# Gate/up of a decoder trunk in float32 halves: one product for both parts of h, sums on ACT and DVE; first scores on 64 rows; mask on the diagonal

## The chip, the cores and the metric

One core of a Trainium2 chip runs the kernel. The metric is device microseconds of one execution, the median of several runs. Engines are written as in the profile: PE (TensorE, matmul), PEld (its weight load), DVE (VectorE), ACT (ScalarE), POOL (GpSimd), SP (SyncE, which issues most DMAs).

## What is computed

A trunk of two layers on 256 tokens of width 1024. Each layer is half-step SwiGLU FFN, token mixer, half-step SwiGLU FFN; the mixer of the first layer is MoBA attention with a relative bias, that of the second is MLA attention. Every sub-layer has an RMS norm and a shift, a scale and a gate that come from `c`.

```python
def swiglu(h, w_gate, w_up, w_down):
    return (jax.nn.silu(h @ w_gate) * (h @ w_up)) @ w_down

for layer in range(DEPTH):                       # DEPTH = 2
    mods = c_act @ ada_w[layer] + ada_b[layer]   # 9 vectors of D_MODEL = 1024
    sh1, sc1, g1, sh2, sc2, g2, sh3, sc3, g3 = jnp.split(mods, 9, axis=-1)
    h = modulate(rms_norm(x, norm_g[layer, 0]), sh1, sc1)
    x = x + 0.5 * g1[:, None, :] * swiglu(h, ...)        # D_FF = 2816
    h = modulate(rms_norm(x, norm_g[layer, 1]), sh2, sc2)
    mix = moba_attention(h, ...) if layer < N_A_LAYERS else mla_attention(h, ...)
    x = x + g2[:, None, :] * mix
    h = modulate(rms_norm(x, norm_g[layer, 2]), sh3, sc3)
    x = x + 0.5 * g3[:, None, :] * swiglu(h, ...)
```

With 256 keys MoBA has one block, so each query sees all keys up to its own. Its heads are 64 wide, those of MLA 96 (query and key).

## The kernel before

**Numbers in two parts.** Weights arrive as float32 (`raw`), and `split` makes a high part `hi` (ACT, L628) and the rest `lo` (DVE, L629), both of type float32r, 128x1024 at a time. `h` is kept likewise as `hh` and `hl`. A product is three matmuls, high by high, high by low, low by high (`mm3`, L758 to L760), summed in PSUM. Weights stream from memory once, through three `raw` buffers and eight `hi` and `lo` each.

**An FFN** (`ffn`). The first 512 of the 2816 hidden columns are done with tokens as output rows and 512 moving weight columns (L905; in the first FFN of all, a routine `first` does 768 columns in its own way). The others go in blocks of 128 hidden columns ("blocks" from here on): the weights are the stationary operand, `h` of all 256 tokens moves, and gate and up of one block fill the two halves of one PSUM buffer `mm` (L934 to L940, with `mm3` once for each of 8 slices `k` of the width). There are 16 such blocks in the first FFN and 18 in each of the other three. `units` then takes SiLU of gate (ACT, L887), multiplies by up (DVE, L888) and splits the result into `gh` and `gl` (L773, L774). Down follows, in two halves of 512 output columns, with `gh`, `gl` stationary.

**Adaptation** (`ada_cols`, `ada_gate`). The shift, scale and gate vectors need 160 tiles of 128x1024 (`adaw`, three buffers), each loaded by SP and taken by one DVE operation: L639 for shift and scale, L677 for gates. They run beside everything else.

**Attention** (`attention`). Four heads at a time. MoBA: q and k are transposed; `qz` holds q for even and odd heads apart, with zeros on the other head's 64 rows, so that a score product runs over 128 rows (L989). Scores of 128 queries by 128 or 256 keys are written side by side into PSUM, bias is added and the row maximum found (L1003), then exponentials, transposition, and the product with v (L1045). MLA: the mask is put into PSUM first by a product of `ident_b` and `masks[t]` (L987), 512 columns, and the scores add to it.

**PSUM.** Eight buffers of 128x512: four `mm`, three `tr` (transpositions and attention, name `at`), one `ada`.

**What sets the order.** The program is written in one order, with attention steps and adaptation interleaved by a clock that `pe` advances. Then `Order` re-arranges each engine's queue: it plays the program through with a duration for each instruction (`duration`) and takes on each engine the ready one that is needed first; on PE it takes program order, except for what has been ready long. The queues on the chip run in the order so found, each engine strictly in its own.

The profiled line numbers are those of the functions below.

Of the kernel before, what the change touches and what calls it, by code (L numbers as in the profile page):

```python
# [197 lines left out]
def duration(i, aps):  # L198
# [5 lines left out]
    if e == "PE":  # L204
# [3 lines left out]
        if i.is_transpose:  # L208
            c = 109.0
        elif dt == F32R:  # L210
            c = max(256, cols) / 2.4 + 13.3
        elif dt == F32:
            c = 114.0 if aps[-1].ap[0][1] == DH else 2 * max(112.0, cols / 1.2 + 2.5)
        else:
            c = max(29.0, cols / 2.4 + 7.0)
# [307 lines left out]
def trunk(ctx: ExitStack, tc: tile.TileContext, a: dict, out: bass.AP):  # L523
# [305 lines left out]
    def split_h(h, c0, n, z):  # L829
        cs = slice(c0, c0 + n)  # L830
        h[2].update(range(c0 // P, (c0 + n) // P))
        return split_evac(h[0][:, cs], h[1][:, cs], z)
# [9 lines left out]

    def new_h(t):
        if t == 0:
            pair[:] = [hp.tile([P, NT, D], F32R, tag=g, name=nm(g)) for g in ("hh", "hl")]
        return pair[0][:, t, :], pair[1][:, t, :], set(), list(pair)

    def hk(h, k):
        until(lambda: k in h[2])
        return kslice(h[0], k), kslice(h[1], k)  # L850

    def hk_both(h, k):
        for t in range(NT):
            until(lambda: k in h[t][2])
        return [x[:, :, k * P:(k + 1) * P] for x in h[0][3]]
# [20 lines left out]
    def ffn(layer, idx, h, after, ada_to, start=None):  # L876

        last = (layer, idx) == (1, 1)
        with ExitStack() as st:
# [4 lines left out]
            def units(f, ps):  # L884

                g = gp.tile([P, NT, P], F32, tag="gT", name=nm("g"), bufs=2)
                nc.scalar.activation(g, ps[:, 0], AF.Silu)  # L887
                nc.vector.tensor_tensor(g, ps[:, 1], g, op=ALU.mult)  # L888
                gh, gl = [gq.tile([P, NT, P], F32R, tag=f"{nme}{f}", name=nm(nme)) for nme in ("gh", "gl")]
                split_evac(gh, gl, g)  # L890
                for t in range(NT):
                    gT[f, t] = gh[:, t, :], gl[:, t, :]

            if start:
                start(units)
# [3 lines left out]
            for t in range(0 if start else NT):  # L899
# [10 lines left out]
                g = gp.tile([P, FB], F32, tag="g", name=nm("g"), bufs=2)  # L910
# [13 lines left out]
            for f0 in range(B1 * P if start else FB, F, S):  # L924
# [45 lines left out]
    UNITS = [(0, [0, 1, 2, 3]), (1, [0, 1]), (1, [2, 3])]  # L970

    def attention(ap, g, qTs, kTs, vs, bias, oT, state, after_s=None):
# [4 lines left out]
        pT, ss, sms = {}, [], []  # L977

        def scores():
            until(lambda: state.get("av", 0) >= g)  # L980
            banks = []
            for t, es in UNITS:
                nk = P * (t + 1)
                ps = at_tile()
                ps3 = ps.rearrange("p (e k) -> p e k", k=nk)
                if bias is None:
                    nc.tensor.matmul(ps, ident_b, masks[t], start=True, stop=False)  # L987
                for i, e in enumerate(es):
                    nc.tensor.matmul(ps3[:, i, :], qTs(e, t), kTs(e, nk), start=bias is not None,  # L989
                                     stop=bias is not None or i == len(es) - 1)  # L990
                banks.append(ps3)
            pe(3.0)
            mxs = []
            for (t, es), ps3 in zip(UNITS, banks):
# [3 lines left out]
                if bias is None:  # L998
                    nc.vector.tensor_reduce(mx[:, :len(es)], ps3, axis=AX.X, op=ALU.max, negate=True)
                else:  # L1000
                    for i, e in enumerate(es):
                        s2, ps2 = [x[:, i, :].rearrange("p (b c k) -> p b c k", c=P // NB, k=NB) for x in (s3, ps3)]
# [4 lines left out]
            for u, (t, es) in enumerate(UNITS):  # L1007
                sm = small([P, 4], "sm")
                for i in range(len(es)):
                    nc.scalar.activation(ss[u][:, i, :], (banks if bias is None else ss)[u][:, i, :], AF.Exp,  # L1010
# [614 lines left out]
```

## Time and profile before

| | |
|---|---|
| runs | 1011.45, 1012.14, 1011.46 us; median 1011.46 |
| the profiled execution: span from first to last instruction | 1009.8 us |
| PE / DVE / ACT / POOL busy | 997.3 / 805.0 / 586.9 / 83.7 us |
| DMA | 260.65 MB, 258 GB/s on average |
| first FFN / MoBA / second FFN | about 0 to 225 / 225 to 335 / 335 to 530 us |
| third FFN / MLA / last FFN | about 530 to 714 / 714 to 820 / 820 to 1009 us |

The profile's only clock is that span; the time of a run also holds what lies around it, here 1.7 us against the median. "Busy" counts an instruction from start to end; matmuls overlap each other, so their cost is read from the distance of their starts.

### The profile page before, as it was taken

What the parts mean: (1) busy time and instruction counts of PE and PEld (TensorE: products, weight loads), DVE (VectorE), ACT (ScalarE), POOL (GpSimd) and SP (SyncE); (2) the same over time, 40 slices, a digit from 0 to 9 for tenths busy, and PEclk for the clock granted to TensorE, in tenths of its full rate; (3) what the DMA queues carried; (4) which work ended last, traced back from release to release, by engine and by line L of the source; (5) the groups of instructions that cost most, each with busy time, mean ns of one, the idle gap of its engine ahead of it and who ended that gap; (6) DMA issues with size and microseconds to landing.
All of it is one profiled execution on the core that took longest, in us unless ns stands there. A gap on an engine that the chain in (4) does not pass through costs nothing.

```text
span 1009.8 us, 17261 instructions
## 1 busy us (share of the span) xinstructions
PE 997.3 (99%) x6678; PEld 899.6 (89%) x6678; DVE 805.0 (80%) x1303; ACT 586.9 (58%) x1029; POOL 83.7 (8%) x124
## 2 busy tenths in 40 slices
PE   8999999999999999999999999999999999999998
PEld 6999998888888799998888999988888889999986
DVE  8999988799888999888799886544998788555542
ACT  5688454378765855455367555543879695555421
POOL 3011000022230000000000000000143010000000
PEclk9999999999999999999999999999999999999999
DMA  9989999899787599998988985562343467544630
GB/s 353 403 294 319 384 336 344 284 338 336 268 287 249 217 330 367 324 315 314 340 321 323 339 298 180 176 210 104 105 151 126 167 247 283 180 167 168 221 133 21
DMA packets 54243, 260.65 MB, mean 258 GB/s; under 512 B 6289, under 2 KB 6801, under 8 KB 35986
## 3 DMA queue, kind: packets, MB, share of 16 engines
q1 hardware_dynamic: 52850, 256.06, 69.6%
q0 software_dynamic: 1024, 3.17, 1.1%
q8 instruction: 52, 0.85, 0.3%
q10 hardware_dynamic: 288, 0.33, 0.1%
q14 instruction: 29, 0.24, 0.1%
HBM read 255.34 MB, written 4.19 MB: 257 GB/s over the span
## 4 chain that ended last, share of the span: by engine, by line
PE 91%; DVE 5%; DMA 2%; ACT 0%; issue 0%; SPq 0%; POOL 0%; DVEq 0%; ACTq 0%
PE mm L758 28%; PE mm L759 27%; PE mm L760 27%; PE at L989 2%; DMA raw<-in_first_dram 1%; PE at L1045 1%; PE at L1025 1%; DVE lo L629 1%; PE tr L1146 1%; PE tr L808 1%; DMA adaw<-in_ada_dram 1%; DVE adaw L639 0%; DVE z L824 0%; DVE wlo L1564 0%; DVE hv L1080 0%
## 5 line engine op out<-in xcount | busy, mean ns | idle before, releaser
L629 DVE TENSOR_TENSOR lo<-raw,hi 128x1024 fp32r<-128x1024 f32 (+3 forms) x312 | 370.8, 1202 | 120.2 <-ACT hi L628 119.6
L628 ACT ACTIVATE hi<-raw 128x1024 fp32r<-128x1024 f32 (+3 forms) x312 | 321.2, 1040 | 178.2 <-PE mm L760 126.0
L759 PE MATMUL mm<-hl,hi 128*128 128x256 f32 x1120 | 314.4, 283 | 0.0
L760 PE MATMUL mm<-hh,lo 128*128 128x256 f32 x1120 | 314.0, 283 | 0.0
L758 PE MATMUL mm<-hh,hi 128*128 128x256 f32 x1120 | 313.3, 284 | 0.0
L759 PEld LDWEIGHTS mm<-hl,hi 128*128 128x128 f32 x1120 | 214.2, 192 | 0.5
L760 PEld LDWEIGHTS mm<-hh,lo 128*128 128x128 f32 x1120 | 213.8, 192 | 0.8 <-DVE lo L629 0.2
L758 PEld LDWEIGHTS mm<-hh,hi 128*128 128x128 f32 x1120 | 213.0, 192 | 1.0 <-ACT hi L628 0.2
L639 DVE CUSTOM_DVE_ANT_0 adaw<-adaw,c_b,cols 128x1024 f32<-128x1024 f32 x112 | 140.5, 1281 | 0.7 <-DMA adaw<-in_ada_dram 0.7
L758 PE MATMUL mm<-hi,gh 128*128 128x512 f32 x352 | 137.4, 390 | 0.0
L760 PE MATMUL mm<-hi,gl 128*128 128x512 f32 x352 | 137.1, 390 | 0.0
L759 PE MATMUL mm<-lo,gh 128*128 128x512 f32 x352 | 137.1, 389 | 0.0
L758 PE MATMUL mm<-hi,hh 128*128 128x512 f32 (+1 forms) x240 | 94.7, 400 | 0.6 <-ACT hh L773 0.6
L760 PE MATMUL mm<-hi,hl 128*128 128x512 f32 (+1 forms) x240 | 92.4, 392 | 1.6 <-DVE hl L774 1.6
L887 ACT ACTIVATE g<-mm 128x256 f32<-128x256 f32 x74 | 28.1, 382 | 112.8 <-PE mm L760 112.8
L759 PE MATMUL mm<-lo,hh 128*128 128x512 f32 (+1 forms) x240 | 92.8, 392 | 0.0
L760 PEld LDWEIGHTS mm<-hi,gl 128*128 128x128 f32 x352 | 66.1, 188 | 13.7
L758 PEld LDWEIGHTS mm<-hi,gh 128*128 128x128 f32 x352 | 66.1, 188 | 13.2
L759 PEld LDWEIGHTS mm<-lo,gh 128*128 128x128 f32 x352 | 66.1, 188 | 13.2
L677 DVE SCALAR_TENSOR_TENSOR acc<-adaw,cols,acc 128x1024 f32<-128x1024 f32 x48 | 61.8, 1288 | 0.1
L888 DVE TENSOR_TENSOR g<-mm,g 128x256 f32<-128x256 f32 x74 | 31.2, 421 | 29.6 <-ACT g L887 29.5
L760 PEld LDWEIGHTS mm<-hi,hl 128*128 128x128 f32 x240 | 45.1, 188 | 10.5 <-DVE hl L774 2.1
(226 smaller groups left out, 1216.7 us busy)
## 6 DMA issues: line engine op xcount, KB each, us to landing
raw<-in_w_dram SPq DMA_DIRECT2D x142, 1024.0 KB, 6.0
adaw<-in_ada_dram SPq DMA_DIRECT2D x160, 512.0 KB, 6.0
raw<-in_first_dram SPq DMA_DIRECT2D x24, 256.0 KB, 7.7
raw<-in_w_dram SPq DMA_DIRECT2D x12, 512.0 KB, 3.5
raw<-in_w_dram SPq DMA_DIRECT2D x6, 576.0 KB, 3.7
bias_d<-bt SPq DMA_DIRECT2D x12, 256.0 KB, 5.0
bg<-bias_d POOLq DMA_DIRECT2D x4, 768.0 KB, 6.5
raw<-in_w_dram SPq DMA_DIRECT2D x2, 768.0 KB, 4.4
```

Of the source, the lines that this page charges most:

```text
L628: nc.scalar.activation(hi, src, AF.Copy)
L629: nc.vector.tensor_tensor(lo, src, hi.bitcast(F32), op=ALU.subtract)
L639: nc.vector.tensor_tensor_reduce(wt, wt, c_b, 1.0, cols[:, i, c:c + 1], op0=ALU.mult, op1=ALU.add, accum_out=m_cols[:, i, c:c + 1])
L677: nc.vector.scalar_tensor_tensor(acc, ada_tile(j, k), cact[:, k:k + 1], acc, op0=ALU.mult, op1=ALU.add)
L758: nc.tensor.matmul(ps, lh, rh, start=start, stop=False)
L759: nc.tensor.matmul(ps, lh, rl, start=False, stop=False)
L760: nc.tensor.matmul(ps, ll, rh, start=False, stop=stop)
L808: nc.tensor.transpose(kslice(pt, j), kslice(y, j), ident)
L887: nc.scalar.activation(g, ps[:, 0], AF.Silu)
L888: nc.vector.tensor_tensor(g, ps[:, 1], g, op=ALU.mult)
L989: nc.tensor.matmul(ps3[:, i, :], qTs(e, t), kTs(e, nk), start=bias is not None, stop=bias is not None or i == len(es) - 1)
L1025: nc.tensor.transpose(kslice(pt, i * (t + 1) + kb), ss[u][:, i, kb * P:(kb + 1) * P], ident)
```

## The change

Five things are done together.

1. `h` becomes one tile `[P, KD, 2, NT, P]`: for each slice `k` the high part of all 256 tokens and then the low part, 512 columns in a row. In a block the high weights meet all 512 at once (L955), so that the left half of a PSUM buffer gets high by high and the right half high by low; then the low weights meet the high part of `h` and add to the right half (L962). Gate and up now have a PSUM buffer each. ACT copies the right half out (L966), DVE adds the left half (L967).
2. In all FFNs but the first, two blocks share a tile `both`: SiLU (L969), product (L970) and split are done once for the pair, on 512 columns. In the first FFN blocks stay single, and their tile is `ry`, of which there is one.
3. The first scores (MoBA): `qz` and its zeros are gone; q and k of a head are read from their own 64 partitions, so a product runs over 64 rows. Scores of even and odd heads go to different PSUM buffers (`sides`), four in all; the fourth is the `ada` buffer. Softmax groups are (0, 2) and (1, 3) instead of (0, 1) and (2, 3).
4. MLA: the mask is one tile of four 128x128 diagonals, added behind the scores and only on the diagonal block.
5. `duration` counts an fp32 product as single when its rows or its output partitions are at most 64, as double otherwise, and `Order` plans with that and with the new program.

```diff
+    def views(x, t):
+        return x[:, :, 0, t, :], x[:, :, 1, t, :], set(), x
+
     def new_h(t):
         if t == 0:
-            pair[:] = [hp.tile([P, NT, D], F32R, tag=g, name=nm(g)) for g in ("hh", "hl")]
-        return pair[0][:, t, :], pair[1][:, t, :], set(), list(pair)
+            pair[:] = [hp.tile([P, KD, 2, NT, P], F32R, tag="h", name=nm("h"))]
+        return views(pair[0], t)
...
+            def unit(f, ps):
+                g = tp.tile([P, S], F32, tag="y", name=nm("g"), bufs=4).rearrange("p (n t q) -> p n t q", n=1, t=NT)
+                nc.scalar.activation(g[:, 0], ps[:, 0], AF.Silu)
+                nc.vector.tensor_tensor(g[:, 0], ps[:, 1], g[:, 0], op=ALU.mult)
+                units(f, g)
...
+                n = 1 if start else 2
                 for f in range(f0 // P, (f0 + S) // P):
-                    ps = mm_tile().rearrange("p (i t q) -> p i t q", i=2, q=P)
+                    j = (f - f0 // P) % n
+                    if not j:
+                        both = (tp.tile([P, 512], F32, tag="ry", name=nm("ry"), bufs=1) if start else
+                                sumsp.tile([P, 1024], F32, tag="both", name=nm("both")))
+                        both = both.rearrange("p (i n t q) -> p i n t q", i=2, t=NT, q=P)
                     for i, pl in enumerate(parts):
+                        ps = mm_tile()
                         for k in range(KD):
                             if len(pl) <= k:
                                 pl += nextw()
-                            mm3(ps[:, i], *[w[:, f * P - f0:(f + 1) * P - f0] for w in pl[k]],
-                                *hk_both(h, k), start=k == 0, stop=k == KD - 1)
+                            wh = pl[k][0][:, f * P - f0:(f + 1) * P - f0]
+                            nc.tensor.matmul(ps, wh, hk_both(h, k).rearrange("p i t q -> p (i t q)"),
+                                             start=k == 0, stop=False)
+                            pe(0.227)
...
-                    units(f, ps)
+                        for k in range(KD):
+                            wl = pl[k][1][:, f * P - f0:(f + 1) * P - f0]
+                            nc.tensor.matmul(ps[:, S:], wl, hk_both(h, k)[:, 0].rearrange("p t q -> p (t q)"),
+                                             start=False, stop=k == KD - 1)
+                            pe(0.12)
+                        sums = both[:, i, j].rearrange("p t q -> p (t q)")
+                        nc.scalar.activation(sums, ps[:, S:], AF.Copy)
+                        nc.vector.tensor_tensor(sums, sums, ps[:, :S], op=ALU.add)
+                    if j == n - 1:
+                        nc.scalar.activation(both[:, 0], both[:, 0], AF.Silu)
+                        nc.vector.tensor_tensor(both[:, 0], both[:, 0], both[:, 1], op=ALU.mult)
+                        units(f - j, both[:, 0], n)
...
+                sides = [at_tile() for _ in range(3)] + [ps_ada.tile([P, 512], F32, tag="ada", name=nm("at"))]
+                sides = [x.rearrange("p (e k) -> p e k", k=P * (i // 2 + 1)) for i, x in enumerate(sides)]
+                for t in range(NT):
+                    for e in range(GH):
+                        nc.tensor.matmul(sides[2 * t + e % 2][:, e // 2, :], qTs(e, t), kTs(e, P * (t + 1)),
+                                         start=True, stop=True)
...
+                    for i, e in enumerate(es):
+                        nc.tensor.matmul(ps3[:, i, :], qTs(e, t), kTs(e, P * (t + 1)), start=i == 0, stop=False)
+                    nc.tensor.matmul(ps3[:, :, t * P:], ident_b, mask[:, :len(es)], start=False, stop=True)
...
+                def half(x, e, n0, n1):
+                    return x[e % 2 * DH:(e % 2 + 1) * DH, e // 2, n0:n1]
```

**PE, gate/up in the first FFN.** One block's gate, as PE's queue holds it before: three matmuls of 256 columns for each `k` (out, then moving operand and weights).

```order
L758 MATMUL mm_1566<-hh_109,hi_1112 128x256
L759 MATMUL mm_1566<-hl_110,hi_1112 128x256
L760 MATMUL mm_1566<-hh_109,lo_1113 128x256
L758 MATMUL mm_1566<-hh_109,hi_1112 128x256
L759 MATMUL mm_1566<-hl_110,hi_1112 128x256
```

In the changed kernel the gate of a block and the start of its up (x4 stands for four such instructions in a row):

```order
L955 MATMUL mm_1558<-h_108,hi_1410 128x512 x4
L955 MATMUL mm_1558<-h_108,hi_1414 128x512 x4
L962 MATMUL mm_1558<-h_108,lo_1411 128x256 x4
L962 MATMUL mm_1558<-h_108,lo_1415 128x256 x4
L955 MATMUL mm_1593<-h_108,hi_1561 128x512 x4
L955 MATMUL mm_1593<-h_108,hi_1565 128x512 x4
```

Eight wide matmuls come first, then eight of 256 with the low weights, and up is in another buffer than gate.

**DVE, the same FFN.** Before, around two blocks (`g` is a block's product, `gl` the low part of it, `acc` a gate tile of adaptation, `lo` a weight half):

```order
L888 TENSOR_TENSOR g_1376<-mm_1219,g_1376 128x256
L774 TENSOR_TENSOR gl_1216<-g_1212,gh_1215 128x256
L629 TENSOR_TENSOR lo_1633<-raw_1626,hi_1632 128x1024
L1298 TENSOR_SCALAR rt_cos<-ang 128x32
L888 TENSOR_TENSOR g_1559<-mm_1383,g_1559 128x256
L774 TENSOR_TENSOR gl_1380<-g_1376,gh_1379 128x256
```

In the changed kernel, one block (`ry` is its sums tile):

```order
L967 TENSOR_TENSOR ry_1557<-ry_1557,mm_1558 128x256
L677 SCALAR_TENSOR_TENSOR acc_1581<-adaw_1730,cols,acc_1581 128x1024
L967 TENSOR_TENSOR ry_1557<-ry_1557,mm_1593 128x256
L1356 TENSOR_TENSOR cosk<-rw_cos,cols 128x16 x2
L970 TENSOR_TENSOR ry_1557<-ry_1557 128x256
L677 SCALAR_TENSOR_TENSOR acc_1581<-adaw_1762,cols,acc_1581 128x1024
L629 TENSOR_TENSOR lo_1716<-raw_1713,hi_1715 128x1024
L774 TENSOR_TENSOR gl_1628<-ry_1557,gh_1627 128x256
L629 TENSOR_TENSOR lo_1720<-raw_1713,hi_1719 128x1024
```

A block has two additions (L967) ahead of its product, with adaptation tiles and weight halves between its steps, and the next block's first addition comes behind its `gl`.

**PE, the scores of MoBA's first four heads.** Before (`at` are the PSUM buffers):

```order
L760 MATMUL mm_3170<-hi_3173,hl_2864 128x512
L989 MATMUL at_3223<-kT_3184,qz 128x128 x4
L989 MATMUL at_3228<-kT_3184,qz 128x256 x2
L989 MATMUL at_3231<-kT_3184,qz 128x256 x2
L758 MATMUL mm_3170<-hi_3173,hh_2863 128x512
```

In the changed kernel, where `at_3036` and `at_3038` take even heads, `at_3037` and `at_3039` odd ones:

```order
L760 MATMUL mm_2984<-hi_2987,h_2681 128x512
L1024 MATMUL at_3036<-kT_2998,qT 128x128
L1024 MATMUL at_3039<-kT_2998,qT 128x256
L1024 MATMUL at_3037<-kT_2998,qT 128x128
L758 MATMUL mm_2984<-hi_2987,h_2681 128x512
L1024 MATMUL at_3036<-kT_2998,qT 128x128
L1024 MATMUL at_3037<-kT_2998,qT 128x128
L1024 MATMUL at_3038<-kT_2998,qT 128x256 x2
L1024 MATMUL at_3039<-kT_2998,qT 128x256
L759 MATMUL mm_2984<-lo_2988,h_2681 128x512
```

Even and odd heads stand partly in turn, and a full-width matmul of the running projection has come between them.

More of the change, by code (lines that the diff above doesn't have):

```diff
@@ L212, in duration @@
         elif dt == F32:
-            c = 114.0 if aps[-1].ap[0][1] == DH else 2 * max(112.0, cols / 1.2 + 2.5)
+            c = (2 if aps[-1].ap[0][1] > DH and aps[0].ap[0][1] > DH else 1) * max(112.0, cols / 1.2 + 2.5)
         else:
@@ L882, in ffn, with units @@
             gq = gp
[L884 to L889, printed above, removed]
-                split_evac(gh, gl, g)
-                for t in range(NT):
-                    gT[f, t] = gh[:, t, :], gl[:, t, :]
+            def units(f, g, n=1):
+                gh, gl = [gq.tile([P, n, NT, P], F32R, tag=f"{nme}{f}", name=nm(nme)) for nme in ("gh", "gl")]
+                split_evac(gh, gl, g)
+                for i in range(n):
+                    for t in range(NT):
+                        gT[f + i, t] = gh[:, i, t, :], gl[:, i, t, :]
+            def unit(f, ps):
[3 more added lines that the diff above has]
+                units(f, g)
             if start:
-                start(units)
+                start(unit)
+            if not start:
+                sumsp = st.enter_context(tc.tile_pool(name=nm("sums"), bufs=2))
             ada_pace(ada_to, 90.0 if last else FFN_PACE, 40.0 if start else 0.0)
@@ L1020, in transposes @@
         def transposes():
-            for u, (t, es) in enumerate(UNITS):
+            for u, (t, es) in enumerate(us):
                 pt = at_tile()
@@ L1049, in av @@
             pov = po.rearrange("p r t q -> p t r q")
-            hi, lo = [x[:, :, kk * P:(kk + 2) * P].rearrange("p t (r q) -> p t r q", q=P) for x in oT[0][3]]
+            hi, lo = [oT[0][3][:, kk:kk + 2, i].rearrange("p r t q -> p t r q") for i in range(2)]
             split_evac(hi, lo, pov)
@@ L1307, in trunk @@
     gcols, tabs = [], []
-    masks = [cp.tile([P, 4 * P], BF16, name=f"mask{t}") for t in range(NT)]
+    mask = cp.tile([P, 4, P], BF16, name="mask")
     def mla_consts():
@@ L1327, in mla_consts @@
             tabs.append(tb)
-        for t in range(NT):
-            m4 = masks[t].rearrange("p (e k) -> p e k", k=P * (t + 1))
-            nc.gpsimd.memset(masks[t], 0.0)
-            nc.gpsimd.affine_select(m4, m4, pattern=[[0, 4 // (t + 1)], [-1, P * (t + 1)]],
-                                    compare_op=ALU.is_ge, fill=NEG, base=t * P, channel_multiplier=1)
+        nc.gpsimd.memset(mask, 0.0)
+        nc.gpsimd.affine_select(mask, mask, pattern=[[0, 4], [-1, P]], compare_op=ALU.is_ge, fill=NEG, base=0,
+                                channel_multiplier=1)
     def rope_apply(ap, dst, src, shape, CG, SG):
@@ L1554, in first @@
                     nc.scalar.activation(z, xT[k], AF.Identity, scale=col_slice(1, key, k, 1), bias=col_slice(0, key, k, 1))
-                    hh, hl = [x[:, :, k * P:(k + 1) * P] for x in h0[0][3]]
+                    hh, hl = [h0[0][3][:, k, i] for i in range(2)]
                     split_evac(hh, hl, z.rearrange("p (t q) -> p t q", q=P))
@@ L1597, in q_norm @@
         hkv[t] = (*(adap.tile([P, D], F32R, tag="acc" if t and g else "adaw", name=nm("hkv"), bufs=1 if t and g else 3)
-                    for g in range(2)), set())
+                    .rearrange("p (k q) -> p k q", q=P) for g in range(2)), set())
         hnext[t] = norm_T(t, (1, 1), ("kv", hkv[t]))
```

59 lines of the change are left out of this document (26 added, 33 removed).

## The prediction

> **What bounds the kernel now.** I read the page's busy shares and the chain that ended last, then busy time by stage, then single matmuls. The three rows below are busy time, VectorE's (DVE's) busy tenths in 40 slices, and the chain's shares by engine.
>
> ```profile
> PE 997.3 (99%) x6678; PEld 899.6 (89%) x6678; DVE 805.0 (80%) x1303; ACT 586.9 (58%) x1029; POOL 83.7 (8%) x124
> ...
> DVE  8999988799888999888799886544998788555542
> ...
> PE 91%; DVE 5%; DMA 2%; ACT 0%; issue 0%; SPq 0%; POOL 0%; DVEq 0%; ACTq 0%
> ```
>
> TensorE (PE) is fed 99% of the span and carries 91% of the chain: time taken from its stream is time taken from the end, as long as somebody can keep up with a faster PE. DVE is the one to watch: above 80% in nearly all of the first 22 slices, half empty at the end. By stage (columns: stretch and its length, busy time and instructions of PE, PEld, DVE, ACT, POOL, then granted clock, DMA share, GB/s):
>
> ```profile
> 60.00:100.00 40.00, 40.00 (x540) 39.23 (x539) 39.05 (x89) 35.17 (x72) 8.02 (x8) 1.00 0.86 293
> 100.00:140.00 40.00, 40.00 (x332) 39.84 (x331) 37.48 (x70) 19.51 (x32) 1.49 (x2) 1.00 0.94 359
> ...
> 240.00:325.00 85.00, 85.00 (x498) 71.03 (x497) 76.62 (x162) 57.22 (x122) 18.12 (x9) 1.00 0.78 271
> ...
> 355.00:450.00 95.00, 95.00 (x775) 94.14 (x774) 85.37 (x115) 48.97 (x70) 1.53 (x2) 1.00 0.93 334
> ...
> 540.00:630.00 90.00, 90.00 (x722) 88.56 (x721) 74.23 (x99) 46.37 (x64) 0.00 (x0) 1.00 0.78 281
> ...
> 714.00:760.00 46.00, 42.36 (x253) 37.04 (x252) 44.73 (x125) 35.36 (x93) 15.12 (x14) 1.00 0.37 125
> ...
> 840.00:910.00 70.00, 70.00 (x584) 69.92 (x583) 44.71 (x55) 34.08 (x49) 0.00 (x0) 1.00 0.55 202
> ```
>
> Gate/up of the four FFNs lies in rows 1 and 2, row 4, row 5 and row 7. PE is never idle there, at full clock; DVE is at 98% and 94% in the first, 90% in the second, 82% in the third, 64% in the last. Only 714 to 760 (start of MLA) is DVE's own.
>
> **Gate/up on PE.** The four rows at 130 us are a gate/up step of three, the next four a down projection with 512 moving columns, in the same type (start, length, instruction); the last is the group's count.
>
> ```profile
> 130.07 0.28 PE L758 MATMUL mm<-hh,hi 128*128 128x256 f32 x1
> 130.19 0.28 PE L759 MATMUL mm<-hl,hi 128*128 128x256 f32 x1
> 130.31 0.28 PE L760 MATMUL mm<-hh,lo 128*128 128x256 f32 x1
> 130.43 0.28 PE L758 MATMUL mm<-hh,hi 128*128 128x256 f32 x1
> ...
> 480.58 0.39 PE L758 MATMUL mm<-hi,gh 128*128 128x512 f32 x1
> 480.80 0.39 PE L759 MATMUL mm<-lo,gh 128*128 128x512 f32 x1
> 481.03 0.39 PE L760 MATMUL mm<-hi,gl 128*128 128x512 f32 x1
> 481.26 0.39 PE L758 MATMUL mm<-hi,gh 128*128 128x512 f32 x1
> ...
> L759 PE MATMUL mm<-hl,hi 128*128 128x256 f32 x1120 | 314.4, 283 | 0.0
> ```
>
> Matmuls overlap, so the cost is from start to start: 120 ns at 256 columns, 226.7 ns (0.68 us for three) at 512. 256 columns more cost 106.7 ns, so each instruction has about 13.3 ns that no column explains. The change turns 120 + 120 + 120 into 226.7 + 120: 13.3 ns a step, 1120 steps, **14.9 us**. By FFN: 256 steps (16 blocks x 2 x 8) in the first, 3.4 us; 288 in each other, 3.8 us.
>
> The Trainium skill ("TensorE: Matmul & The Clock Gate", section "Back-to-back issue gap") gives the spacing as columns over 2.4 GHz plus about 2.5 ns, which makes the merger worth 2.5 ns a step, 2.8 us in all. The rows above disagree with that and decide for the sum; the case stays among the rivals.
>
> **First scores.** Rows: the 16 score instructions of one group and the matmuls after them; then the attention-times-V product, 24 instructions on 64 of the array's columns, in alternating halves; then two pieces of the chain for scores of MLA, which pack nothing (start, us, count).
>
> ```profile
> 244.60 2.78 PE L989 MATMUL at<-kT,qz 128*128 128x128 f32 x16
> 247.03 0.58 PE L758 MATMUL mm<-hi,hh 128*128 128x512 f32 x1
> 247.45 0.40 PE L759 MATMUL mm<-lo,hh 128*128 128x512 f32 x1
> ...
> 257.51 1.58 PE L1045 MATMUL at<-pT,v 128*64 128x128 f32 x24
> 259.02 0.50 PE L758 MATMUL mm<-hi,hh 128*128 128x512 f32 x1
> ...
> 763.06 0.89 PE at L989 x8
> 764.17 0.86 PE at L989 x4
> ```
>
> Scores take 2.43 us, and the first wide matmul after them needs 0.42 us instead of 0.23, so a group costs 2.62 us: 111 ns an instruction at 128 columns (0.89 over 8), 215 at 256, two instructions a product. The products in column halves run at 63 ns (1.51 over 24) instead of 111, so two halves do run at once. No row shows halves of 64 rows. Bounds: no overlap and one more change of shape on each side, 0.2 us lost a group, 0.8 in all; perfect overlap, 1.31 us won a group, 5.2 in all. I take a value inside by walking the new order as the column halves behave (a product waits for its own half; even heads use the upper 64 rows, odd ones the lower): an even product at 128 beside an odd one at 256, another odd at 128 behind it (0.65 us); a wide matmul; then an even and an odd at 128 (0.22), an even at 256 alone (0.43), an even and an odd at 256 (0.43). That is 1.73 us, plus the 0.19 us behind the scores, now paid a second time around the wide matmul in the middle: about 2.0 us, 0.6 won a group, **2.4 us** in four groups (PE is never idle between 240 and 325 us). [...] One copy of q on ACT instead of two is off the path, and so are the dropped POOL memsets.
>
> **Mask on diagonals.** One mask product of 512 columns and the scores behind it:
>
> ```profile
> 762.67 0.39 PE L987 MATMUL at<-mask,ident_b 128*128 128x512 bf16 x1
> 762.89 1.06 PE L989 MATMUL at<-kT,qT 96*128 96x128 f32 x8
> ```
>
> 0.22 us for 512 columns. Two of a group's three products fall to 256: 0.22 us a group, 0.9 in four. One or two groups fall into the stretch that DVE ends, so **0.6 us** counts.
>
> **What is added to DVE and ACT.** The prices (mean ns of one), and below them starts that show what an operation occupies when others queue behind it:
>
> ```profile
> L629 DVE TENSOR_TENSOR lo<-raw,hi 128x1024 fp32r<-128x1024 f32 x296 | 358.5, 1223 | 117.7 <-ACT hi L628 117.1
> L639 DVE CUSTOM_DVE_ANT_0 adaw<-adaw,c_b,cols 128x1024 f32<-128x1024 f32 x112 | 140.5, 1281 | 0.7 <-DMA adaw<-in_ada_dram 0.7
> L773 ACT ACTIVATE gh<-g 128x256 fp32r<-128x256 f32 x76 | 31.0, 409 | 17.1 <-DVE g L888 17.0
> L887 ACT ACTIVATE g<-mm 128x256 f32<-128x256 f32 x74 | 28.1, 382 | 112.8 <-PE mm L760 112.8
> ...
> 132.58 0.42 DVE L888 TENSOR_TENSOR g<-mm,g 128x256 f32<-128x256 f32 x1
> 132.92 2.43 DVE L629 TENSOR_TENSOR lo<-raw,hi 128x1024 fp32r<-128x1024 f32 x2
> 135.26 0.42 DVE L888 TENSOR_TENSOR g<-mm,g 128x256 f32<-128x256 f32 x1
> ...
> 714.98 0.69 DVE L866 TENSOR_TENSOR x<-x,ry 128x512 f32<-128x512 f32 x1
> 715.59 0.41 DVE L824 TENSOR_SCALAR y<-tr,m_cols 128x128 f32<-128x128 f32 x1
> ```
>
> DVE is held 0.34 us by 256 columns, 0.61 by 512, 1.17 by a weight half. Each block now has two additions, and a pair has one product and one difference of 512 for two each of 256. First FFN (blocks single): 2 x 0.34 x 16 = 10.9 us. Elsewhere a pair goes from 1.36 to 2.58 us: 1.22 x 27 = 33 us, 11 an FFN. DVE rises from 805 to about 849 us. ACT gains two copies a block, 140 at 0.38 us or 53 us at most, and has room (58%).
>
> Two rows on the column tiles of adaptation (`L639`, two records a tile):
>
> ```profile
> 540.00:630.00 90.00, 20.04 (x32) 1.00 0.78 281
> 630.00:714.00 84.00, 0.00 (x0) 1.00 0.48 164
> ```
>
> Where is DVE's cover? Adaptation tiles (1.28 us each), which fill its gaps ahead of need. The new order has six fewer of them done by the 32nd and by the 128th weight half: 7.7 us handed back, and third and fourth FFN have 18% and 36% free. So late gate/up counts in full. The early ones don't: in the first, DVE had 76.53 of 80 us and gets 10.9 more in a stretch that should shrink by 3.4; minus 7.7 it is full. I count its 3.4 us as not won. In the second, 85.4 + 11 stands against 95 - 3.8, so DVE has to give up four tiles to stay level, and its additions now wait for ACT's copies in a queue without slack: I count half, 1.9 us. Behind a waiting addition on DVE's queue stand the weight halves, for which PE waits; and adaptation tiles whose buffers SP's next load needs, with weights behind it on SP. That is why a full DVE would show as PE waiting for `lo` or for a PSUM buffer. Four PSUM buffers now hold two blocks, not four; at 2.77 us a half block that leaves 8 us for evacuation.
>
> **Sum.** 14.9 + 2.4 + 0.6 - 3.4 - 1.9 = 12.6 us. The profiled execution's span is 1009.8 us, the median 1011.46, so 1.7 lie around it. 1011.5 - 12.6 = **998.9 us**, its own range 993 to 1004.
>
> **Rivals.** (1) All is won: DVE hands back enough tiles, half-row scores overlap fully. 14.9 + 5.2 + 0.9 = 21 us, 990.5. For it: PE had no idle time even where DVE stood at 98%. Chance 0.13. (2) DVE bounds everything up to 540 us; only third and fourth FFN and the mask pay, 7.7 + 0.6: 1003.2, up to 1009 if its queue loses a few us more. For it: 90 to 98% busy before 11 us are added per FFN. Against: the 20 us of column tiles in 540 to 630 us are the last two vectors, used only behind MLA, so earlier tiles can still move back. Chance 0.18. (3) Slower: in the first FFN all blocks share one sums buffer, `ry`, so copy, addition, SiLU, product and split of a block (2.05 us from the up half's end) must end before the next block's first copy. PE needs 5.55 us a block. DVE's row in the new order holds per block two additions, a product, a difference, two weight halves and one adaptation tile, 4 x 0.34 + 2 x 1.17 + 1.28 = 5.0 us, without a wait. With 0.8 us of waits too many a block the 12.6 us are gone; with one more 1.2 us operation ahead in each, 16 x 1.2 = 19 us, 1018. Against: ready work can fill those waits. Chance 0.11. (4) The 13.3 ns go with every 256 moving columns and not with the instruction, so that the merged matmul takes 240: scores and mask alone pay, 1011.5 - 3.0 = 1008.5, near 1010 with added waits. Against: the down rows, 227 for 512 columns. Chance 0.04. The Trainium skill's spacing formula, named above, leans to this case. Forecast: 0.54.
>
> A measurement of this kernel tells about 0.2% (2 us) from nothing. Slower is (3) and a tail of (2), 0.11; same is the rest of (2) and (4) above 1009.4, 0.06; faster 0.83. The range 990 to 1008 leaves out the slow case and the tails.
>
> **What would show it.** Right: 512-column starts 227 ns apart at the merged line, 256 at 120; 70 blocks with two more DVE and ACT operations; score groups near 2.0 us; PE above 98%; DVE near 849 us and above 95% up to 540 us. Wrong: PE waiting on additions or `lo` in 60 to 150 or 355 to 450 us (then (2) or (3)), merged starts near 240 ns (4), scores at 2.6 us or more.

## The result: 6.1 us faster, half of what was forecast

The changed kernel takes 1005.32 us in the median of four runs (1004.79 to 1006.99), the kernel before 1011.8 in the runs beside it. The ratio is 0.9938, 95% interval 0.9924 to 0.9952: 0.5 to 0.8% faster. Against the 1011.46 that the prediction started from, 6.1 us were won; 12.6 were forecast. The profiled execution (1006.99 us, span 1005.2) is the longest of the four.

From the page of the changed kernel: busy time, and three groups of gate/up (wide products, narrow products, DVE's additions; count, busy time, mean ns of one, idle time ahead).

```profile
PE 986.0 (98%) x5558; PEld 834.1 (83%) x5558; DVE 844.9 (84%) x1389; ACT 616.7 (61%) x1111; POOL 83.8 (8%) x120
...
L955 PE MATMUL mm<-h,hi 128*128 128x512 f32 x1120 | 288.3, 394 | 2.5 <-DVE ry L967 1.8
...
L962 PE MATMUL mm<-h,lo 128*128 128x256 f32 x1120 | 162.0, 283 | 0.0
...
L967 DVE TENSOR_TENSOR both<-both,mm 128x256 f32<-128x256 f32 x108 | 44.9, 416 | 14.4 <-ACT both L966 14.0
```

DVE rose by 40 us (805 to 845; 849 was forecast), and PE still waits for gate/up's sums only 1.8 us in all. Nothing here shows where six of the 12.6 us went. For that I cut both traces at the start of each stage's last residual (`x<-x,ry` on DVE). Stage lengths in us, worked out from those rows; "gate/up only" and "old price" are experiments told below:

| stage | before | changed | gate/up only | old price |
|---|---|---|---|---|
| up to the end of the first FFN | 220.7 | 220.0 | 217.8 | 219.6 |
| MoBA | 119.2 | **121.8** | 119.5 | 115.4 |
| second FFN | 187.7 | 185.2 | 184.6 | 185.4 |
| third FFN | 187.4 | 184.4 | 184.4 | 184.4 |
| MLA | 104.4 | **106.1** | 104.4 | 105.6 |
| fourth FFN | 186.4 | 183.7 | 183.7 | 183.7 |

The FFNs won 8.9 us. MoBA and MLA, for which 3.0 us of gain stood in the sum, lost 4.3. (The first row also holds the start of the program. In the eight profiled kernels with the same gate/up it ended anywhere between 216.3 and 220.0, at 218.1 on average, so one column alone says little about it.)

**Gate/up as a half block.** Three rows of the third FFN, a half block and the start of the next (start, length, instruction and count):

```profile
570.51 2.00 PE L955 MATMUL mm<-h,hi 128*128 128x512 f32 x8
572.35 1.11 PE L962 MATMUL mm<-h,lo 128*128 128x256 f32 x8
573.30 2.00 PE L955 MATMUL mm<-h,hi 128*128 128x512 f32 x8
```

Eight wide products take 1.84 us to the next start, eight narrow ones 0.95: 2.79 for 24 x 0.12 = 2.88 before. The starts of half blocks lie 2.79 or 2.80 us apart, 2.793 on average. That is 0.087 us less a half block, 12.2 us over 140 of them, where the prediction had 14.9 gross. Eight at 226.7 ns and eight at 120 would be 2.77.

**A score group of MoBA in the changed kernel:**

```profile
244.66 0.39 PE L760 MATMUL mm<-hi,h 128*128 128x512 f32 x1
244.97 0.92 PE L1024 MATMUL at<-kT,qT 64*128 64x128 f32 x6
245.83 0.50 PE L758 MATMUL mm<-hi,h 128*128 128x512 f32 x1
246.26 1.35 PE L1024 MATMUL at<-kT,qT 64*128 64x128 f32 x10
247.54 0.50 PE L759 MATMUL mm<-lo,h 128*128 128x512 f32 x1
247.87 0.39 PE L760 MATMUL mm<-hi,h 128*128 128x512 f32 x1
```

From 244.66 to 247.87, less the three wide products at 0.227 each, a group costs 2.53 us. By the same count (from 244.37 to 247.45, two wide products) it cost 2.63 before. The other three groups, counted so, give 2.54 to 2.56. Only 0.1 us is won, and a wide product stands in the middle; a group without it is shown below.

**The end of MoBA in the changed kernel.** First the end of the out projection and what follows on PE; then the same stretch by windows (length; busy time and count of PE, PEld, DVE, ACT, POOL; granted clock, DMA share, GB/s):

```profile
332.09 0.39 PE L760 MATMUL mm<-hi,oT 128*128 128x512 f32 x1
334.02 0.84 PE L808 MATMUL tr<-ident,y 128*128 128x128 f32 x4 [1.55 <-ACT y L803]
335.41 0.55 PE L758 MATMUL mm<-hi,h 128*128 128x512 f32 x1 [0.55 <-ACT h L773]
335.76 0.63 PE L759 MATMUL mm<-lo,h 128*128 128x512 f32 x1
336.19 0.63 PE L758 MATMUL mm<-hi,h 128*128 128x512 f32 x1
```

```profile
333.00:336.00 3.00, 1.43 (x6) 0.93 (x7) 2.97 (x4) 2.78 (x8) 0.07 (x1) 0.95 0.11 46
336.00:339.00 3.00, 3.00 (x9) 2.23 (x9) 3.00 (x6) 1.70 (x6) 0.00 (x0) 0.50 1.01 325
```

The same place in the kernel before:

```profile
332.97 0.84 PE L808 MATMUL tr<-ident,y 128*128 128x128 f32 x4 [0.19 <-ACT y L803]
334.36 0.50 PE L758 MATMUL mm<-hi,hh 128*128 128x512 f32 x1 [0.56 <-ACT hh L773]
...
336.00:339.00 3.00, 3.00 (x17) 2.42 (x16) 2.96 (x7) 2.85 (x9) 0.00 (x0) 1.00 1.03 423
```

Two things are new in the changed kernel. PE waits 1.55 us instead of 0.19 for `y`, the scaled rows that open the next norm. And then wide products start 0.43 us apart instead of 0.23: the granted clock is 0.50. Read in windows of 1 us, the drop lasts 3.4 us (335.7 to 339.1), so about 1.7 us are lost. So the questions for the experiments were: is gate/up or the scores to blame for MoBA's end, and what made MLA longer?

### The profile page after: what moved, and what is told of

It is laid out like the page before. It is cut to its first block, busy times and chain, and to the rows that moved or that the text cites. A ratio compares the mean times of both kernels' runs of the same rounds, so it can differ in the third digit from the quotient of the medians.

```text
span 1005.2 us, 15142 instructions
## 1 busy us (share of the span) xinstructions
PE 986.0 (98%) x5558; PEld 834.1 (83%) x5558; DVE 844.9 (84%) x1389; ACT 616.7 (61%) x1111; POOL 83.8 (8%) x120
## 4 chain that ended last, share of the span: by engine, by line
PE 76%; issue 11%; DMA 6%; DVE 5%; ACT 2%; POOL 1%; SPq 0%; POOLq 0%; ACTq 0%; DVEq 0%
PE mm L955 20%; PE mm L758 13%; PE mm L759 13%; PE mm L760 13%; PE mm L962 11%; DMA adaw<-in_ada_dram 2%; DMA bias_d<-bt 2%; DMA raw<-in_first_dram 1%; PE at L1081 1%; DVE lo L629 1%; PE at L1016 1%; PE at L1024 1%; PE tr L808 1%; DMA raw<-in_w_dram 1%; PE at L1061 1%
## 5 line engine op out<-in xcount | busy, mean ns | idle before, releaser
L955 PE MATMUL mm<-h,hi 128*128 128x512 f32 x1120 | 288.3, 394 | 2.5 <-DVE ry L967 1.8
L955 PEld LDWEIGHTS mm<-h,hi 128*128 128x128 f32 x1120 | 199.7, 189 | 37.8 <-DVE ry L967 2.1
L962 PEld LDWEIGHTS mm<-h,lo 128*128 128x128 f32 x1120 | 155.3, 190 | 11.9
L962 PE MATMUL mm<-h,lo 128*128 128x256 f32 x1120 | 162.0, 283 | 0.0
L966 ACT ACTIVATE both<-mm 128x256 f32<-128x256 f32 x108 | 40.6, 376 | 91.0 <-PE mm L962 90.6
L758 PE MATMUL mm<-hi,h 128*128 128x512 f32 (+1 forms) x240 | 94.9, 401 | 0.8 <-ACT h L773 0.8
L760 PE MATMUL mm<-hi,h 128*128 128x512 f32 (+1 forms) x240 | 93.5, 394 | 1.6 <-DVE h L774 1.6
L759 PE MATMUL mm<-lo,h 128*128 128x512 f32 (+1 forms) x240 | 94.9, 397 | 0.0
L967 DVE TENSOR_TENSOR both<-both,mm 128x256 f32<-128x256 f32 x108 | 44.9, 416 | 14.4 <-ACT both L966 14.0
L760 PEld LDWEIGHTS mm<-hi,h 128*128 128x128 f32 x240 | 45.5, 190 | 10.4 <-DVE h L774 2.1
L758 PEld LDWEIGHTS mm<-hi,h 128*128 128x128 f32 x240 | 45.4, 189 | 9.7 <-ACT h L773 1.3
L759 PEld LDWEIGHTS mm<-lo,h 128*128 128x128 f32 x240 | 45.3, 189 | 9.0 <-issue 1.0
```

The costliest lines, as they stand in the source:

```text
L758: nc.tensor.matmul(ps, lh, rh, start=start, stop=False)
L759: nc.tensor.matmul(ps, lh, rl, start=False, stop=False)
L760: nc.tensor.matmul(ps, ll, rh, start=False, stop=stop)
L955: nc.tensor.matmul(ps, wh, hk_both(h, k).rearrange("p i t q -> p (i t q)"), start=k == 0, stop=False)
L962: nc.tensor.matmul(ps[:, S:], wl, hk_both(h, k)[:, 0].rearrange("p t q -> p (t q)"), start=False, stop=k == KD - 1)
L966: nc.scalar.activation(sums, ps[:, S:], AF.Copy)
```

## Experiments

All times are medians beside runs of the kernel before on the same chip (1011.3 to 1011.4).

**Gate/up alone, and one edit undone at a time.** The first kernel has the old scores (`qz` on 128 rows) and the old masks; the next two undo one of these edits each.

```diff
-  nc.tensor.matmul(sides[2 * t + e % 2][:, e // 2, :], qTs(e, t), kTs(e, P * (t + 1)), ...)   # 64 rows
+  nc.tensor.matmul(ps3[:, i, :], qTs(e, t), kTs(e, P * (t + 1)), ...)                         # qz, 128 rows
-  nc.tensor.matmul(ps3[:, :, t * P:], ident_b, mask[:, :len(es)], start=False, stop=True)     # behind the scores
+  nc.tensor.matmul(ps, ident_b, masks[t], start=True, stop=False)                             # ahead of them, 512 wide
```

> The changed kernel with the old scores (zero-padded q, 128 rows) and the old full-width masks, so that only gate/up is changed. By the last residuals of the stages gate/up won 8.9 us, while MoBA lost 2.6 and MLA 1.7. Theory A (the new scores and masks themselves cost these stages 4.3 us, by breaks and by another order of work): MoBA and MLA get back to their old lengths (119.2 and 104.4 us between residuals), the time is 1011.5 - 8.9 = 1002.6, faster than the changed kernel by 2 to 4 us. Theory B (the scores and masks earn the 3.0 us forecast, and the loss comes from the fuller DVE and ACT queues that gate/up hands on): the time is 1005.3 + 3.0 = 1008.3, and MoBA's end still waits about 1.5 us for `y`.

> The changed kernel with the old scores on 128 rows only; masks and gate/up stay new. Theory A (the new scores pay nothing, and MoBA's 2.6 us went because of them): MoBA is 119.2 us again instead of 121.8, the time about 1002.7. Theory B (the scores earn 2.4 us, the fuller queues cost MoBA 5): MoBA grows to about 124, the time about 1007.7. Either way a score group takes 2.6 us and the wait for `y` at MoBA's end tells which.

> The changed kernel with the old full-width masks only. Theory A (the masks' move behind the scores lets the planner put the first MLA score group earlier, with a 1.3 us wait for ACT behind it): MLA is 104.4 us again instead of 106.1, the time about 1003.6. Theory B (the masks earn 0.6 to 1.3 us, the wait comes from elsewhere): MLA is 106.5 to 107.5 us, the time 1006 to 1006.6.

| scores \ masks | old | new |
|---|---|---|
| old (128 rows) | 1000.82 (0.9896, 0.9882 to 0.9909) | 998.33 (0.9871, 0.9858 to 0.9885) |
| new (half rows) | 1004.12 (0.9926, 0.9913 to 0.9938) | 1005.32 (0.9938, 0.9924 to 0.9952) |

Theory A holds for the scores, more strongly than I had written: gate/up alone wins 10.6 us, and the half-row scores cost 3.3 us with the old masks and 7.0 with the new. For the masks theory A of the third kernel came out too (MLA 104.2 us, 1004.1). They win 2.5 us with the old scores; the 1.2 that they lose with the new ones lie within the noise of the times, but the traces show a longer MLA (106.1 against 104.2). Two of these kernels make a clean pair, since their first FFNs end 0.04 us apart (217.76 and 217.72): gate/up only (first fence) and the one with old masks and half-row scores (second).

```profile
329.79 0.39 PE L760 MATMUL mm<-hi,oT 128*128 128x512 f32 x1
330.36 0.84 PE L808 MATMUL tr<-ident,y 128*128 128x128 f32 x4 [0.19 <-ACT y L803]
331.75 0.50 PE L758 MATMUL mm<-hi,h 128*128 128x512 f32 x1 [0.56 <-ACT h L773]
```

```profile
329.74 0.39 PE L760 MATMUL mm<-hi,oT 128*128 128x512 f32 x1
331.68 0.84 PE L808 MATMUL tr<-ident,y 128*128 128x128 f32 x4 [1.54 <-ACT y L803]
333.06 0.79 PE L758 MATMUL mm<-hi,h 128*128 128x512 f32 x1 [0.55 <-ACT h L773]
```

PE ends MoBA's products at the same moment in both. With half-row scores `y` is 1.35 us late, and the halved clock follows. The lateness stands on DVE: the first residual of the out projection starts at 322.73 in the first kernel and at 325.41 in the second, and `y` needs all residuals of its rows.

```profile
322.73 0.69 DVE L868 TENSOR_TENSOR ry<-mm,gate 128x512 f32<-128x512 f32 x1 [1.23 <-PE mm L760]
```

```profile
325.41 0.69 DVE L868 TENSOR_TENSOR ry<-mm,gate 128x512 f32<-128x512 f32 x1 [0.17 <-PE mm L760]
```

Each waits for the last product of its accumulator on PE. PE's last attention-times-V products are over as much later (321.47 against 318.77), and two wide products stand between them. So it is the order of PE's work that moved, not DVE's load.

**A second sums buffer in the first FFN.** The two halves of a block get a `y` buffer each (four of them) instead of sharing one `ry`.

```diff
-  both = (tp.tile([P, 512], F32, tag="ry", ..., bufs=1) if start else ...)
+  if start: both = [tp.tile([P, S], F32, tag="y", ..., bufs=4) ... for _ in range(2)]
```

> The changed kernel with two pairs of sums buffers in the first FFN instead of one. Theory A (the single buffer makes the 1.8 us wait for the addition and 0.8 us wait for `hi`; the first FFN won 0.7 of 3.4 us for that): the 2.6 us come back, the first FFN ends 2 to 2.6 us earlier, the time is about 1003. Theory B (DVE is full there, 38.1 to 39.2 us of every 40, and another buffer gives it no time): the waits only move, the first FFN ends within 0.7 us of before, the time 1005 +- 1.

Measured 1005.12 (0.993, 0.9917 to 0.9944). The waits between 45 and 160 us went from 1.8 + 0.8 to 0.5 + 0.8 us. The first FFN of the profiled execution ended 1.2 us earlier (218.8), between the two theories and inside the spread of kernels that share one buffer, and the time did not move beyond the noise. Gate/up only, which has the one buffer, waits just the 0.8. So the buffer costs about a microsecond at most, not the 12 of rival 3, which fell.

**The half-row scores on the kernel before, and the planner's price.** The change also edits one line of the planner's table of durations. It prices a half-row product at one pass (112 or 216 ns) where a full one had two. I put that price back, all instructions staying as they are. (The line also halves two one-row products at the very start of the program. The four residuals of the first FFN lie 0.4 us apart in the two profiled executions, so those two don't carry the difference.)

```diff
-  c = (2 if aps[-1].ap[0][1] > DH and aps[0].ap[0][1] > DH else 1) * max(112.0, cols / 1.2 + 2.5)
+  c = (2 if aps[-1].ap[0][1] > DH else 1) * max(112.0, cols / 1.2 + 2.5)
```

> The kernel before with the half-row scores alone; gate/up and masks stay old. With gate/up new, they cost 3.3 us (1004.1 against 1000.8) or 7.0 us (1005.3 against 998.3). Theory A (the half-row scores cost by themselves: a group is no shorter in place, all three transposes' banks and the adaptation's one are taken at once, and the out projection's residuals come later): 1014 to 1018, MoBA about 121.5 us between residuals instead of 119.2, and a wait for `y` of 1 us or more at its end. Theory B (they cost only where gate/up has filled DVE's queue): 1009 to 1012, MoBA 119 us or less.

> The changed kernel, its instructions all the same, but the planner prices a half-row product as it did a full one (224 or 430 ns instead of 112 or 216). Only the order can change. Theory A (the loss is an order that the lower price picked): 998 to 1001, no wait over 0.3 us for `y` at MoBA's end and no drop of the granted clock behind it. Theory B (the loss is in the work itself: breaks around the groups, four banks at once): 1004 to 1006, the wait for `y` and the drop stay.

The half-row scores alone on the kernel before: 1014.37, slower (1.0027, 1.0016 to 1.0038). MoBA took 121.7 us, PE waited 2.1 us for `y`, and the clock was halved behind it. The changed kernel with the old price: **999.0** (0.9877, 0.9863 to 0.989), 6.3 us faster than with the new price, by order alone. Theory A's numbers came out in both; for the first kernel its reason (the products cost by themselves) did not, since the same products gain at the old price, as shown further down. A score group in the old-price kernel, and its end of MoBA by windows:

```profile
244.21 0.39 PE L760 MATMUL mm<-hi,h 128*128 128x512 f32 x1
244.53 1.58 PE L1024 MATMUL at<-kT,qT 64*128 64x128 f32 x16
246.04 0.50 PE L758 MATMUL mm<-hi,h 128*128 128x512 f32 x1
246.37 0.40 PE L759 MATMUL mm<-lo,h 128*128 128x512 f32 x1
```

```profile
330.00:333.00 3.00, 2.72 (x13) 2.03 (x12) 3.00 (x6) 2.94 (x10) 0.00 (x0) 1.00 0.67 218
333.00:336.00 3.00, 3.00 (x16) 2.48 (x15) 2.96 (x7) 2.97 (x8) 0.00 (x0) 1.00 0.98 396
```

The sixteen instructions stand together. By the count used above the group costs 1.71 us, 0.92 less than before, and a wide product in its middle costs 0.82 us. The second and third group cost 1.72 or 1.73, the last, whose sixteen instructions take 0.32 us longer, 2.04. MoBA takes 115.4 us instead of 121.8. The 6.4 us follow from the rows: 3.0 in the four groups, 1.35 to 1.55 of wait for `y`, 0.27 less wait for `h`, and 1.7 of clock, 6.3 to 6.5 in all.

Why the low price splits a group stays open. The planner's rule for PE is to take what is earliest in the program among instructions that were ready 400 ns ago, and in the changed kernel a wide product comes in when three products, to three different banks, have been issued; no run tests the link.

**The same with the old gate/up, the price alone, and the masks under the old price.** The first kernel is the one with half-row scores alone, at the old price. In the second the scores are on 128 rows and only their price is halved. The third is the old-price kernel with the old masks.

> The kernel before with the half-row scores alone (as `scores_only`, 1014.4), but the planner's price for their products left as it was. With gate/up new, the old price kept the 16 products of a group together: a group then costs PE 1.71 us instead of 2.63, and MoBA took 115.4 us. Theory A (half-row scores earn 0.92 us a group when nothing is put between them, whatever gate/up does): MoBA 115.5 us, the time 1011.4 - 3.7 = 1007.7. Theory B (the gain needs the new gate/up, or comes from another stage): 1010 to 1012.

> The changed kernel with the old scores on 128 rows (998.3), and the planner prices their products at half, as the change does for half rows: again the order alone changes. Theory A (the low price does harm by putting a wide product into the middle of a half-row group and so delaying the out projection; groups of 128 rows have all products ready together and stay whole): 997.5 to 999.5, groups of 2.78 us in one piece. Theory B (any too low price delays the out projection's residuals): a wait for `y` of 1 us or more and a clock drop at MoBA's end, 1001 to 1002.

> The changed kernel with the planner's old price for half-row products (999.0) and the old full-width masks. In `old_price` MLA still took 105.6 us, with waits of 1.1 us for `s` and 0.8 for `kn`; with old masks and the low price it was 104.2. Theory A (that order of MLA goes with the new masks when the scores are half-row): MLA 104.2, the time 997.6, the fastest yet. Theory B (it goes with the rest of the order): MLA 105.5 or more, the time 999 to 1000.

Half-row scores at the old price on the kernel before: 1008.1 (0.9968, 0.9956 to 0.998), MoBA 115.3 us, as theory A said: 3.2 us are earned without the new gate/up. The low price on 128-row scores: 1000.46 (0.9898, 0.9884 to 0.9912), 2.1 us more than at the old price and 1 us above theory A's range. Theory B's signs are absent: no wait for `y`, the clock full at MoBA's end. Three of the four groups stayed whole; the last was split, but so it is at the old price. A wait of 1.8 us for `ckT` came up in MLA instead of 0.7. A wrong price costs something by itself, but most of the harm needs half rows:

| scores, with new gate/up and new masks | old price | low price |
|---|---|---|
| 128 rows | 998.33 | 1000.46 |
| half rows | 999.0 | 1005.32 |

The old price with the old masks: **997.4** (0.9863, 0.9849 to 0.9876), the fastest of all, as theory A said, with MLA at 104.2 us. So at the old price half-row scores win 3.4 us with the old masks (1000.8 to 997.4) and nothing clear with the new ones (998.3 to 999.0). Rows of MLA in the changed kernel: the first score products on PE and the transposes that wait; then ACT in between:

```profile
747.68 1.05 PE L1016 MATMUL at<-kT,qT 96*128 96x128 f32 x8
753.76 1.08 PE L1453 MATMUL tr<-ident,qn 128*96 128x128 f32 x8 [1.27 <-ACT s L1046]
```

```profile
749.27 1.06 ACT L628 ACTIVATE hi<-raw 128x1024 fp32r<-128x1024 f32 x1 [0.71 <-DMA raw<-in_w_dram]
750.34 1.28 ACT L1046 ACT_TABLE_LOAD   x1
751.64 0.37 ACT L1046 ACTIVATE s<-at,mx 128x128 f32<-128x128 f32 x1
```

A weight half (1.06 us) goes ahead of the table load and the exponentials on ACT. With the old masks (and half-row scores) the table load comes first, and the exponentials start 2.1 us behind the first score product (747.33 and 745.22). The exponentials read the scores out of the PSUM buffers that PE's transposes need next. But the weight half alone is not the loss: with the new masks and the old scores, where MLA takes 103.9 us, it stands ahead as well:

```profile
740.84 1.06 ACT L628 ACTIVATE hi<-raw 128x1024 fp32r<-128x1024 f32 x1 [0.31 <-DMA raw<-in_w_dram]
...
743.21 0.37 ACT L1044 ACTIVATE s<-at,mx 128x128 f32<-128x128 f32 x1
...
745.33 1.08 PE L1458 MATMUL tr<-ident,qn 128*96 128x128 f32 x8 [0.32 <-DVE kn L1492]
```

There the exponentials start 3.0 us behind the first score product (740.21), in the changed kernel 4.0, and PE waits 0.3 us instead of 1.3. The weights' data came later in the changed kernel (ACT waited 0.71 us for them, not 0.31); what else makes the difference was not tested.

**Gate/up's changes of width.** On the kernel with the old scores and new masks (998.33), the narrow product of each k right behind its wide one, and then the reverse: 16 wide, 16 narrow.

```diff
   for k in range(KD):  matmul(ps, wh, h of both tokens' parts); 
+      matmul(ps[:, S:], wl, high part of h)            # interleaved: here
-  for k in range(KD):  matmul(ps[:, S:], wl, ...)      # grouped: here, per half; coarse: after both halves
```

> The changed kernel with the old scores (998.3) and, in gate/up, the narrow product of each k right behind its wide one instead of eight wide and then eight narrow. A grouped half block takes 2.79 us for 8 x 0.2267 + 8 x 0.12 = 2.77. Theory A (a change of width costs about 10 ns, two of them are the 0.02 us): 16 changes cost 0.16 us a half block, 140 x 0.14 = 20 us more, 1018. Theory B (every product costs its own columns whatever stands beside it, and the 0.02 us belong to the new PSUM bank): within 1 us of 998.3. Theory C (a narrow product hides less of its neighbour's weight load when they alternate): slower by more than 20 us.

> The changed kernel with the old scores (998.3), and in gate/up the wide products of gate and up first (16), then the narrow ones of both (16): half as many changes of width, but both PSUM banks of a block are held to its end and its four evacuations come at once. Theory A (changes of width are the 0.02 us of a half block): 1.4 us less, 996.9. Theory B (they are not, and evacuation has room): 998.3 +- 0.7. Theory C (the late evacuation makes PE wait for banks: two blocks in four banks, 4 operations of 0.34 to 0.38 us behind each other): slower, 1000 or more, with PE waiting for the additions.

Interleaved 1000.12 (0.989, 0.9877 to 0.9904), coarse 999.47 (0.9881, 0.9866 to 0.9896). Rows of the interleaved kernel: the wide products that open a half block and the next one, in the third FFN and in the fourth; then the coarse kernel, a whole block and the next start:

```profile
560.01 0.39 PE L955 MATMUL mm<-h,hi 128*128 128x512 f32 x1
...
562.78 0.39 PE L955 MATMUL mm<-h,hi 128*128 128x512 f32 x1
...
866.05 0.40 PE L955 MATMUL mm<-h,hi 128*128 128x512 f32 x1
...
868.88 0.40 PE L955 MATMUL mm<-h,hi 128*128 128x512 f32 x1
```

```profile
866.21 3.82 PE L956 MATMUL mm<-h,hi 128*128 128x512 f32 x16
869.86 2.08 PE L965 MATMUL mm<-h,lo 128*128 128x256 f32 x16
871.78 3.82 PE L956 MATMUL mm<-h,hi 128*128 128x512 f32 x16
```

With 16 changes of width a half block takes 2.77 us in the third FFN, just its columns, and 2.83 in the fourth. Theory A fell: where nothing else slows the stream, a change of width costs nothing. So did theory B: the third FFN changes PSUM banks as often as before, without the 0.02 us, and the time is 1.8 us off. The third FFN is 1.5 us shorter than in the grouped kernel, of which the missing 0.02 us in 36 half blocks makes 0.7; the second is 1.7 and the fourth 0.6 us longer. What slows these two I did not find. The coarse block takes 5.57 us for 5.55 of columns, so it saves 0.02 us a block as forecast, but PE waits 2.3 us for the additions in the first FFN (theory C), which eats it. Neither order pays.

**Does the pause bring the halved clock?** In the old-price kernel ACT writes the first `y` behind MoBA five times instead of once:

```diff
-  nc.scalar.activation(y, xs[t][:, c0:c0 + n], AF.Copy, scale=r)
+  for _ in range(5 if t == 0 and c0 == 0 and keys[0][0] == (0, 2) else 1):
+      nc.scalar.activation(y, xs[t][:, c0:c0 + n], AF.Copy, scale=r)
```

> The changed kernel with the planner's old price (999.0, no drop of the granted clock), and ACT writes `y` behind MoBA five times over instead of once, so that PE's transposes there wait about 1.4 us longer (4 x 0.34), as they do in the changed kernel. Theory A (the pause itself brings the drop of the granted clock behind it, 8 wide products at 0.43 instead of 0.23 us): 999.0 + 1.4 + 1.7 = 1002.1, granted clock 0.85 to 0.9 in the 12 us behind the pause. Theory B (the pause and the drop are not tied): 1000.4, clock 1.00.

```profile
331.26 0.83 PE L809 MATMUL tr<-ident,y 128*128 128x128 f32 x4 [1.32 <-ACT y L804]
332.65 0.57 PE L758 MATMUL mm<-hi,h 128*128 128x512 f32 x1 [0.55 <-ACT h L773]
333.01 0.63 PE L759 MATMUL mm<-lo,h 128*128 128x512 f32 x1
```

```profile
333.00:336.00 3.00, 3.00 (x8) 2.05 (x7) 3.00 (x8) 2.55 (x8) 0.00 (x0) 0.50 1.00 421
```

Measured 1003.38 (0.9918, 0.9906 to 0.9931): 4.4 us more than without the pause, of which theory A explains 3.1. The longer `y` also changed the plan: the last score group is split here (12 instructions, three wide products, then 4) and by the count above costs 2.99 us instead of 2.04, which is 0.95 of the 1.3 us left. The drop is there, at 0.50. A split group elsewhere (the last one with the old scores) has no drop behind it, so it is the late `y` that brings the halved clock, whatever makes it late.

## What was right in the prediction, and the step that failed

- **Gate/up.** The mechanism was right: wide products 227 ns apart, narrow ones 120. The term was mis-sized twice, in opposite directions. Gross it is 12.2 us, not 14.9, for 0.02 us in each grouped half block that no row of before showed and no run here explained. And the deductions of 3.4 and 1.9 for a full DVE were not due: alone, gate/up won 10.6 us against the 9.5 forecast, with 3.1 in the second FFN, and 2.6 in the first stage on average over the eight kernels with the same gate/up (0.7 to 4.4). DVE was indeed full, busy 79.5 of 80 us between 60 and 140 us with gate/up only, but part of its work could wait: it put adaptation tiles off. Busy time and count of those between 60 and 140 us, in the kernel before and with gate/up only:

```profile
60.00:140.00 80.00, 20.50 (x16) 1.00 0.90 326
```

```profile
60.00:140.00 80.00, 15.33 (x12) 1.00 0.84 297
```

  I had seen this handing back, and still took a full DVE for a bound. In the second FFN DVE took the additions from its idle tenth (85.4 to 92.0 of 95 us). Rivals 2 and 3 fell; so did rival 4. The spacing formula of the Trainium skill ("TensorE: Matmul & The Clock Gate", section "Back-to-back issue gap"), given there for a matmul by itself, leaned to it with 2.8 us gross; the 227 and 120 ns of these streams decide against it here.
- **Scores: the step that failed.** The term gave 0.6 us a group; the changed kernel won 0.1. (My own figures, 1.73 plus twice 0.19, add up to 2.1 us and not 2.0.) The breaks were priced right: around the three wide products 0.08, 0.20 and 0.10 us are lost, 0.38 in all, as twice 0.19. That is luck, since my 0.19 stood behind products on all 128 rows. What failed is the walk of the halves: the two pieces take 0.86 and 1.28 us from their first start to the next wide product, where I had 0.65 and 1.08. A whole group takes 1.51 where perfect overlap had 1.31. So each stretch of half-row products costs 0.2 us that I put at nothing, and a second stretch costs them again; why is not shown. The bigger part of the step: I read the new order as given, and did not ask what an order without the break would be worth, though the line that sets it is part of the change. Whole, a group costs 1.71 us, and four earn 3.3 us, more than the 2.4 that I took.
- **MoBA's end: not in the sum at all.** The same order delays the out projection's residuals, PE waits 1.55 us for `y`, and the clock then stands at half, 1.7 us lost. This is the other half of the failed step: the score term took a change of order to move nothing outside its groups. My "PE waiting" rivals looked only at gate/up's stretches. The halved clock is in no row of before.
- **Masks.** With old scores MLA won 0.5 us (104.35 to 103.87), as forecast (0.6). With half-row scores MLA lost 1.4 to 1.9, of which PE's wait for the exponentials makes 0.9 to 1.3. The other 2 us that the masks won with old scores are not in MLA: in the traces MoBA gets 2.4 us shorter (119.5 to 117.1) and the second FFN 1.5 longer, where no mask is. I did not trace them.
- **The sum.** 9.5 + 2.4 + 0.6 was forecast; 10.6 less 4.5 came (1000.8 to 1005.3). With the old price the kernel takes 999.0, where the forecast was 998.9. That is luck, and of another order than the one forecast: gate/up and whole score groups earn more than their terms, and MLA gives it back.

## What to carry to other kernels

A duration in a scheduler's table is part of the kernel: here one line cost 6.3 us while every instruction stayed the same, so test a re-priced operation apart from the edit that prompted it. Keep half-row products together, and count what an instruction between them costs by the whole group, start to start. A full engine need not be a bound: see whether some of its work can wait, as DVE's adaptation tiles did here. When a stage that was not touched gets longer, look at its last wait and at the granted clock right behind it.

## What the runs showed of the hardware

- **A halved clock behind a short pause.** In all four kernels with half-row scores at the low price, and in the one with the delayed `y`, PE waited 1.3 to 2.1 us, did four transposes, and waited 0.4 to 0.6 us more. About then the granted clock fell to 0.50, for 3.4 us in each of the five (from windows of 1 us). Pauses of 1.3 us in MLA and 1.8 in the first FFN brought no drop. The Trainium skill ("TensorE: Matmul & The Clock Gate", section "What's actually happening") says that the clock falls to half after an idle window of some 3.4 us and comes back after about 3.4 us of work. The half and the length of the drop agree; the pause here was shorter and not idle throughout: 2.9 to 3.7 us without a wide product, with four transposes inside (332.3 to 335.4 us in the changed kernel). Transposes alone don't make the difference: in MLA (752.3 to 756.9 us in the changed kernel) PE had a wait of 1.3 us and twenty transposes and no other product for 4.6 us, and the clock stayed at 1.00. In that stretch PE was busy 2.9 us, behind MoBA 0.84. How much work keeps the clock up stays open.
- **Half-row float32 products** of two heads run at once when they stand together: 16 instructions in 1.51 us (244.53 to 246.04) against 2.43 on 128 rows.
